# A 3-D affine grid: shared table instructions, one store per add, and theta loaded in halves

## Chip, cores, metric

The kernel runs on one core of one Trainium2 chip. The metric is the device time of one execution in microseconds (us). All times quoted are medians; every execution used here was at a granted clock of 1.0. The span of the profile (first to last recorded instruction) is about 1.8 us shorter than the measured time.

## The reference

For each of 8 batches there is a 3x4 matrix theta. The output at depth z, height y, width x is theta times (x, y, z, 1), with all coordinates running from -1 to 1:

```python
batch, d, h, w = 8, 32, 64, 64
grid = stack([xx, yy, zz, ones], axis=-1)           # d, h, w, 4
result[b] = einsum('dhwc,ec->dhwe', grid, theta[b])  # 8, 32, 64, 64, 3 in float32: 12.58 MB
```

The input is 384 bytes, the output 12.58 MB. The work is to write the output.

## The kernel before

The 256 pairs (batch, depth) are the rows of two tiles of 128 partitions, "half 0" (batches 0 to 3) and "half 1" (batches 4 to 7). Within a partition, every output element is a sum of two table entries: `yc[h, e]` (which also holds the depth and the constant term) and `xt[w, e]`. VectorE builds half 0's tables, ScalarE half 1's. Then VectorE adds them with broadcasts, a few rows of `h` at a time, and stores go out on the sync queue (half 0) and the scalar queue (half 1).

```python
for k in range(2):                       # theta, 32 copies of each batch's 12 numbers
    th_in = dataclasses.replace(theta2d, offset=theta2d.offset + 48 * k,
                                ap=[[12, 4], [0, 32], [1, 12]])
    (nc.sync if k == 0 else nc.scalar).dma_start(out=th[:], in_=th_in)
# ... iota, xrow (x coordinates), zc (z coordinate of each partition, in four blocks of 32)
for e in range(E):                       # half 0's tables: nine small instructions
    nc.vector.tensor_scalar(out=zb0[:, e:e+1], in0=zc[:], scalar1=th0[:, 4*e+2:4*e+3],
                            scalar2=th0[:, 4*e+3:4*e+4], op0=MUL, op1=ADD)
for e in range(E):
    nc.vector.tensor_scalar(out=yc0_3[:, :, e], in0=xrow[:, :H], scalar1=th0[:, 4*e+1:4*e+2],
                            scalar2=zb0[:, e:e+1], op0=MUL, op1=ADD)
    nc.vector.tensor_scalar(out=xt0_3[:, :, e], in0=xrow[:], scalar1=th0[:, 4*e:4*e+1], ...)
# ... half 1's tables, the same on nc.scalar
csplit = [2, 2, 4, 8, 8, 8, 8, 8, 8, 8]  # rows of h in each add
dsplit = [2, 2, 4, 16, 16, 16, 8]        # rows of h in each store
for k in range(2):
    for nh in csplit:
        nc.vector.tensor_tensor(out=otv[:, h0:h0+nh], in0=yc3 (broadcast), in1=xt3 (broadcast), op=ADD)
    q = nc.sync if k == 0 else nc.scalar
    for nh in dsplit:
        q.dma_start(out=out2d[k*P:(k+1)*P, ...], in_=ot[:, ...])
```

## Time and profile before

| | before |
|---|---|
| measured time | 43.54 us |
| span of the profile | 41.7 us |
| first table instruction of half 0 | 4.34 us |
| first add | 6.18 us |
| first output byte starts | 7.61 us |
| VectorE ends its last add | about 33.25 us |
| last output byte | 40.54 us |

The first and the last output byte come from the trace's records of single DMA packets; the rest from the views below.

The page of the kernel before, in 40 slices of the span: busy tenths of VectorE and of the 16 DMA engines, and what they moved, and then the count of packets by size.

```profile
DVE  0400899999999999999999999999999800000000
DMA  0000000785048999899998999998998999889960
GB/s 0 0 8 4 0 0 0 249 305 200 0 188 377 377 518 424 377 389 506 424 377 377 430 402 371 390 480 377 471 471 377 377 506 436 377 377 436 412 283 0
DMA packets 2280, 12.60 MB, mean 302 GB/s; under 512 B 488, under 2 KB 1000, under 8 KB 1512
```

The DMA row is nearly full from the 13th slice to the 38th, while VectorE falls idle seven slices before the DMA engines do. So the stores bound the end, though the page's chain of waits (the chain of work that ended last, followed back) puts 65% of the span on VectorE. There is a gap at the start of the DMA row. In windows of 0.5 us (window, length, busy time of VectorE, ScalarE and GpSimd with instruction counts, clock, DMA share, GB/s) it looks like this:

```profile
7.50:8.00 0.50, 0.50 (x1) 0.00 (x0) 0.00 (x0) 1.00 0.75 261
8.50:9.00 0.50, 0.50 (x1) 0.00 (x0) 0.00 (x0) 1.00 0.54 197
...
9.50:10.00 0.50, 0.50 (x2) 0.00 (x0) 0.00 (x0) 1.00 0.85 332
10.00:10.50 0.50, 0.50 (x1) 0.00 (x0) 0.00 (x0) 1.00 0.00 0
...
11.50:12.00 0.50, 0.50 (x1) 0.00 (x0) 0.00 (x0) 1.00 0.00 0
12.00:12.50 0.50, 0.50 (x1) 0.00 (x0) 0.00 (x0) 1.00 0.94 393
```

Nothing moves for 2 us, because the first 16-row store waits for two adds of 8 rows. The timeline of the sync queue shows when it was issued (start in us, length, what), and the queue's own waits come after it (what waited, for what, total, times, longest):

```profile
11.45 0.33 SPq L137 DMA_DIRECT2D out_dram<-ot  x1
```

```profile
SPq L137 <- DVE ot L130: 16.0, 6, 5.3
```

The store before it was issued from 8.11 to 8.44 us, so the queue waited 3.0 us for the two adds.

The start, from the timeline of the kernel before (start in us, length, engine, line, instruction; in brackets the idle time before it and what ended it):

```profile
0.73 0.71 SPq L47 DMA_DIRECT2D th<-in_theta_dram  x1
0.74 1.09 ACTq L47 DMA_DIRECT2D th<-in_theta_dram  x1
...
4.34 0.27 DVE L90 TENSOR_SCALAR xt<-xrow,th 128x64 f32<-128x64 f32 x1 [2.64 <-DMA th<-in_theta_dram]
...
6.18 27.07 DVE L130 TENSOR_TENSOR ot<-yc,xt 128x384 f32<-128x384 f32 x20
```

The chain of waits has theta's landing for VectorE at 0.73 + 3.51 = 4.24 us (start, length, what):

```profile
0.73 3.51 DMA th<-in_theta_dram
```

VectorE waits 2.64 us for theta, then needs 1.84 us for the tables. The adds by shape (the grouped view with shapes kept apart):

```profile
L130 DVE TENSOR_TENSOR ot<-yc,xt 128x1536 f32<-128x1536 f32 x14 | 23.5, 1750 | 0.0
L130 DVE TENSOR_TENSOR ot<-yc,xt 128x384 f32<-128x384 f32 x4 | 2.0, 551 | 0.0
```

By these two shapes an add costs about 0.15 us plus 1.04 ns per element.

### The profile page before, as it was taken

The page shows a single profiled execution, that of the slowest core. Times are in us where ns is not written, and L with a number is a line of the kernel's source. Part 1 is how long each engine was busy: PE and PEld are TensorE (multiplying, and loading weights), DVE is VectorE, ACT ScalarE, POOL GpSimd, SP SyncE. Part 2 cuts the span into 40 slices and gives each one's busy share as a digit, 9 for nine tenths or more (in the row PEclk, how much of TensorE's full clock was granted, in tenths as well). Part 3 has the DMA queues.
Part 4 walks back from the last instruction along what each step waited for, and adds up shares of the span by engine and source line. Part 5 has one row for each costly group of instructions (what it writes and reads, how often), then busy time and mean ns, then how long its engine had stood idle before and what let it go on. Part 6 is the DMA issues. An engine that isn't in the chain of part 4 may idle for free.

```text
span 41.7 us, 122 instructions
## 1 busy us (share of the span) xinstructions
DVE 29.4 (70%) x32; ACT 4.1 (10%) x11; POOL 1.0 (2%) x9
## 2 busy tenths in 40 slices
DVE  0400899999999999999999999999999800000000
ACT  0297990000000000000000000000000000000000
POOL 4500000000000000000000000000000000000000
DMA  0000000785048999899998999998998999889960
GB/s 0 0 8 4 0 0 0 249 305 200 0 188 377 377 518 424 377 389 506 424 377 377 430 402 371 390 480 377 471 471 377 377 506 436 377 377 436 412 283 0
DMA packets 2280, 12.60 MB, mean 302 GB/s; under 512 B 488, under 2 KB 1000, under 8 KB 1512
## 3 DMA queue, kind: packets, MB, share of 16 engines
q1 hardware_dynamic: 1140, 6.30, 36.9%
q10 hardware_dynamic: 1140, 6.30, 36.7%
HBM read 0.01 MB, written 12.58 MB: 302 GB/s over the span
## 4 chain that ended last, share of the span: by engine, by line
DVE 65%; DMA 8%; DVEq 4%; issue 1%
DVE ot L130 61%; DMA th<-in_theta_dram 8%; DVEq L171 4%; DVE yc L86 2%; DVE zb L81 2%; DVE xt L90 1%; DVEq L90 0%
## 5 line engine op out<-in xcount | busy, mean ns | idle before, releaser
L130 DVE TENSOR_TENSOR ot<-yc,xt 128x1536 f32<-128x1536 f32 (+2 forms) x20 | 27.1, 1430 | 0.0
L90 DVE TENSOR_SCALAR xt<-xrow,th 128x64 f32<-128x64 f32 x3 | 0.8, 268 | 2.6 <-DMA th<-in_theta_dram 2.6
L97 ACT ACT_TABLE_LOAD x1 | 1.3, 1283 | 1.9 <-issue 1.9
L109 ACT ACTIVATE yc<-xrow,zb,th 128x64 f32<-128x64 f32 x3 | 1.2, 456 | 0.0
L112 ACT ACTIVATE xt<-xrow,th 128x64 f32<-128x64 f32 x3 | 1.1, 364 | 0.0
L68 DVE TENSOR_SCALAR xrow<-iw 128x64 f32<-128x64 int32 x1 | 0.2, 195 | 1.1 <-POOL iw L53 1.1
L104 ACT ACTIVATE zb<-zc,th 128x1 f32<-128x1 f32 x3 | 0.9, 372 | 0.0
L86 DVE TENSOR_SCALAR yc<-xrow,th,zb 128x64 f32<-128x64 f32 x3 | 0.9, 324 | 0.0
L81 DVE TENSOR_SCALAR zb<-zc,th 128x1 f32<-128x1 f32 x3 | 0.6, 267 | 0.0
L59 POOL TENSOR_SCALAR zc<-ipf 32x1 f32<-32x1 f32 x2 | 0.4, 182 | 0.2
L59 DVE TENSOR_SCALAR zc<-ipf 32x1 f32<-32x1 f32 x2 | 0.3, 147 | 0.1
L97 ACT ACTIVATE warm<-th 128x12 f32<-128x12 f32 x1 | 0.2, 212 | 0.2 <-DMA th<-in_theta_dram 0.2
L55 POOL CAST ipf<-ip 128x1 f32<-128x1 int32 x1 | 0.2, 212 | 0.1
L53 POOL IOTA iw<- 128x64 int32 x1 | 0.2, 181 | 0.0
L51 POOL IOTA ip<- 128x1 int32 x1 | 0.1, 133 | 0.4 <-PEq L171 0.4
L157 POOL MEMSET const-float32-0.0<- 128x1 f32 x1 | 0.1, 99 | 0.2 <-issue 0.2
L157 POOL MEMSET const-bfloat16-1.0<- 128x1 bf16 x1 | 0.1, 102 | 0.0
L157 POOL MEMSET const-uint8-127<- 128x1 uint8 x1 | 0.1, 102 | 0.0
L157 POOL MEMSET const-float32-1.0<- 128x1 f32 x1 | 0.1, 99 | 0.0
## 6 DMA issues: line engine op xcount, KB each, us to landing
out_dram<-ot SPq DMA_DIRECT2D x3, 1536.0 KB, 5.3
out_dram<-ot ACTq DMA_DIRECT2D x3, 1536.0 KB, 7.1
out_dram<-ot SPq DMA_DIRECT2D x1, 768.0 KB, 6.4
out_dram<-ot ACTq DMA_DIRECT2D x1, 768.0 KB, 7.6
out_dram<-ot SPq DMA_DIRECT2D x2, 192.0 KB, 1.9
out_dram<-ot SPq DMA_DIRECT2D x1, 384.0 KB, 2.3
out_dram<-ot ACTq DMA_DIRECT2D x2, 192.0 KB, 6.1
out_dram<-ot ACTq DMA_DIRECT2D x1, 384.0 KB, 6.0
```

The lines of the kernel that those rows point to most:

```text
L53: nc.gpsimd.iota(iw[:], pattern=[[1, W]], base=0, channel_multiplier=0)
L59: eng.tensor_scalar(out=zc[j * D:(j + 1) * D], in0=ipf[j * D:(j + 1) * D], scalar1=2.0 / (D - 1), scalar2=-1.0 - (2.0 * j * D) / (D - 1), ...
L81: nc.vector.tensor_scalar(out=zb0[:, e:e + 1], in0=zc[:], scalar1=th0[:, 4 * e + 2:4 * e + 3], scalar2=th0[:, 4 * e + 3:4 * e + 4], op0=MU ...
L86: nc.vector.tensor_scalar(out=yc0_3[:, :, e], in0=xrow[:, :H], scalar1=th0[:, 4 * e + 1:4 * e + 2], scalar2=zb0[:, e:e + 1], op0=MUL, op1=ADD)
L90: nc.vector.tensor_scalar(out=xt0_3[:, :, e], in0=xrow[:], scalar1=th0[:, 4 * e:4 * e + 1], scalar2=None, op0=MUL)
L97: nc.scalar.mul(out=warm[:], in_=th1[:], mul=1.0)
L104: nc.scalar.activation(out=zb1[:, e:e + 1], in_=zc[:], func=ident, bias=th1[:, 4 * e + 3:4 * e + 4], scale=th1[:, 4 * e + 2:4 * e + 3])
L109: nc.scalar.activation(out=yc1_3[:, :, e], in_=xrow[:, :H], func=ident, bias=zb1[:, e:e + 1], scale=th1[:, 4 * e + 1:4 * e + 2])
L112: nc.scalar.activation(out=xt1_3[:, :, e], in_=xrow[:], func=copyf, bias=0.0, scale=th1[:, 4 * e:4 * e + 1])
L130: nc.vector.tensor_tensor(out=otv[:, h0:h0 + nh], in0=in0, in1=in1, op=ADD)
L157: nc = _bacc.Bacc("TRN2", target_bir_lowering=False, num_devices=1)
L171: with _tile.TileContext(nc) as tc:
```

## The change

The intent was to reach the first store sooner and then never to let the stores run dry. It has three parts: theta in four half loads spread over both queues; five tensor-tensor instructions for half 0's tables in place of nine per-component ones; adds and stores of the same 4 to 9 rows. (It also adds switchable forms of half 1's tables, which are not used, and moves the z coordinate to VectorE.)

```diff
-        th_in = dataclasses.replace(
-            theta2d, offset=theta2d.offset + 48 * k,
-            ap=[[12, 4], [0, 32], [1, 12]])
-        (nc.sync if k == 0 else nc.scalar).dma_start(out=th[:], in_=th_in)
+        for half in range(2):
+            th_in = dataclasses.replace(
+                theta2d, offset=theta2d.offset + 48 * k + 24 * half,
+                ap=[[12, 2], [0, 32], [1, 12]])
+            q = nc.sync if half == 0 else nc.scalar
+            q.dma_start(out=th[64 * half:64 * (half + 1), :], in_=th_in)
 ...
-    (zc by four blocks of 32 partitions, on GpSimd and VectorE)
+    nc.vector.tensor_scalar(out=ipd[:], in0=ip[:], scalar1=D - 1,
+                            scalar2=None, op0=mybir.AluOpType.bitwise_and)
+    nc.vector.tensor_scalar(out=zc[:], in0=ipd[:], scalar1=2.0 / (D - 1),
+                            scalar2=-1.0, op0=MUL, op1=ADD)
 ...
-    (nine tensor_scalar for zb0, yc0, xt0)
+    nc.vector.tensor_tensor(out=xt0_3[:], in0=xrow_he, in1=thcol(th0, 0), op=MUL)
+    nc.vector.tensor_tensor(out=zb0[:], in0=zc_e, in1=(th0, column 2), op=MUL)
+    nc.vector.tensor_tensor(out=zb0[:], in0=zb0[:], in1=(th0, column 3), op=ADD)
+    nc.vector.tensor_tensor(out=yc0_3[:], in0=xrow_he, in1=thcol(th0, 1), op=MUL)
+    nc.vector.tensor_tensor(out=yc0_3[:], in0=yc0_3[:], in1=(zb0, broadcast), op=ADD)
 ...
-    csplit = [2, 2, 4, 8, 8, 8, 8, 8, 8, 8]
-    dsplit = [2, 2, 4, 16, 16, 16, 8]
+    csplit=(4, 4, 4, 4, 5, 5, 6, 7, 8, 9, 8),
+    dsplit=(4, 4, 4, 4, 5, 5, 6, 7, 8, 9, 8),
```

More of the change, by code (lines that the diff above doesn't have):

```diff
@@ L19 @@
     out: bass.AP,
+    csplit=(4, 4, 4, 4, 5, 5, 6, 7, 8, 9, 8),
+    dsplit=(4, 4, 4, 4, 5, 5, 6, 7, 8, 9, 8),
+    k1_mode="scalar",
+    dma_q="alt",
 ):
@@ L53 @@
     nc.gpsimd.iota(iw[:], pattern=[[1, W]], base=0, channel_multiplier=0)
-    ipf = const.tile([P, 1], fp32)
-    nc.gpsimd.tensor_copy(out=ipf[:], in_=ip[:])
+    ipd = const.tile([P, 1], i32)
+    nc.vector.tensor_scalar(out=ipd[:], in0=ip[:], scalar1=D - 1,
+                            scalar2=None, op0=mybir.AluOpType.bitwise_and)
     zc = const.tile([P, 1], fp32)
-    def zc_block(eng, j):
-        eng.tensor_scalar(
-            out=zc[j * D:(j + 1) * D], in0=ipf[j * D:(j + 1) * D],
-            scalar1=2.0 / (D - 1), scalar2=-1.0 - (2.0 * j * D) / (D - 1),
-            op0=MUL, op1=ADD)
-    zc_block(nc.gpsimd, 0)
-    zc_block(nc.gpsimd, 1)
+    nc.vector.tensor_scalar(out=zc[:], in0=ipd[:], scalar1=2.0 / (D - 1),
+                            scalar2=-1.0, op0=MUL, op1=ADD)
     xrow = const.tile([P, W], fp32)
@@ L69 @@
                             scalar2=-1.0, op0=MUL, op1=ADD)
-    zc_block(nc.vector, 2)
-    zc_block(nc.vector, 3)
     tables = []
@@ L79, with thcol @@
     xt0_3 = xt0.rearrange("p (w e) -> p w e", e=E)
-    for e in range(E):
-        nc.vector.tensor_scalar(
-            out=zb0[:, e:e + 1], in0=zc[:],
-            scalar1=th0[:, 4 * e + 2:4 * e + 3],
-            scalar2=th0[:, 4 * e + 3:4 * e + 4], op0=MUL, op1=ADD)
-    for e in range(E):
-        nc.vector.tensor_scalar(
-            out=yc0_3[:, :, e], in0=xrow[:, :H],
-            scalar1=th0[:, 4 * e + 1:4 * e + 2],
-            scalar2=zb0[:, e:e + 1], op0=MUL, op1=ADD)
-        nc.vector.tensor_scalar(
-            out=xt0_3[:, :, e], in0=xrow[:],
-            scalar1=th0[:, 4 * e:4 * e + 1], scalar2=None, op0=MUL)
+    xrow_he = xrow[:, :, None].to_broadcast((P, W, E))
+    def thcol(th, c):
+        return dataclasses.replace(
+            th, offset=th.offset + c, ap=[th.ap[0], [0, W], [4, E]])
+    nc.vector.tensor_tensor(out=xt0_3[:], in0=xrow_he, in1=thcol(th0, 0),
+                            op=MUL)
+    zc_e = zc.to_broadcast((P, E))
+    nc.vector.tensor_tensor(
+        out=zb0[:], in0=zc_e,
+        in1=dataclasses.replace(th0, offset=th0.offset + 2,
+                                ap=[th0.ap[0], [4, E]]), op=MUL)
+    nc.vector.tensor_tensor(
+        out=zb0[:], in0=zb0[:],
+        in1=dataclasses.replace(th0, offset=th0.offset + 3,
+                                ap=[th0.ap[0], [4, E]]), op=ADD)
+    nc.vector.tensor_tensor(out=yc0_3[:], in0=xrow_he, in1=thcol(th0, 1),
+                            op=MUL)
+    nc.vector.tensor_tensor(
+        out=yc0_3[:], in0=yc0_3[:],
+        in1=zb0[:, None, :].to_broadcast((P, W, E)), op=ADD)
     tables.append((yc0_3, xt0_3))
     th1 = ths[1]
-    warm = const.tile([P, 12], fp32)
-    nc.scalar.mul(out=warm[:], in_=th1[:], mul=1.0)
     zb1 = const.tile([P, E], fp32)
@@ L102, with k1_tables_scalar @@
     xt1_3 = xt1.rearrange("p (w e) -> p w e", e=E)
-    for e in range(E):
-        nc.scalar.activation(
-            out=zb1[:, e:e + 1], in_=zc[:], func=ident,
-            bias=th1[:, 4 * e + 3:4 * e + 4],
-            scale=th1[:, 4 * e + 2:4 * e + 3])
-    for e in range(E):
-        nc.scalar.activation(
-            out=yc1_3[:, :, e], in_=xrow[:, :H], func=ident,
-            bias=zb1[:, e:e + 1], scale=th1[:, 4 * e + 1:4 * e + 2])
-        nc.scalar.activation(
-            out=xt1_3[:, :, e], in_=xrow[:], func=copyf,
-            bias=0.0, scale=th1[:, 4 * e:4 * e + 1])
+    def k1_tables_scalar():
+        warm = const.tile([P, 12], fp32)
+        nc.scalar.mul(out=warm[:], in_=th1[:], mul=1.0)
+        for e in range(E):
+            nc.scalar.activation(
+                out=zb1[:, e:e + 1], in_=zc[:], func=ident,
+                bias=th1[:, 4 * e + 3:4 * e + 4],
+                scale=th1[:, 4 * e + 2:4 * e + 3])
+        for e in range(E):
+            nc.scalar.activation(
+                out=yc1_3[:, :, e], in_=xrow[:, :H], func=ident,
+                bias=zb1[:, e:e + 1], scale=th1[:, 4 * e + 1:4 * e + 2])
+            nc.scalar.activation(
+                out=xt1_3[:, :, e], in_=xrow[:], func=copyf,
+                bias=0.0, scale=th1[:, 4 * e:4 * e + 1])
@@ new lines, in k1_tables_vector @@
+    def k1_tables_vector():
+        for e in range(E):
+            nc.vector.tensor_scalar(
+                out=zb1[:, e:e + 1], in0=zc[:],
+                scalar1=th1[:, 4 * e + 2:4 * e + 3],
+                scalar2=th1[:, 4 * e + 3:4 * e + 4], op0=MUL, op1=ADD)
+        for e in range(E):
+            nc.vector.tensor_scalar(
+                out=yc1_3[:, :, e], in0=xrow[:, :H],
+                scalar1=th1[:, 4 * e + 1:4 * e + 2],
+                scalar2=zb1[:, e:e + 1], op0=MUL, op1=ADD)
+            nc.vector.tensor_scalar(
+                out=xt1_3[:, :, e], in0=xrow[:],
+                scalar1=th1[:, 4 * e:4 * e + 1], scalar2=None, op0=MUL)
@@ new lines, in k1_tables_eng @@
+    def k1_tables_eng(eng):
+        th1_he = thcol(th1, 1)
+        nc_e = eng
+        nc_e.tensor_tensor(out=xt1_3[:], in0=xrow_he, in1=thcol(th1, 0),
+                           op=MUL)
+        nc_e.tensor_tensor(
+            out=zb1[:], in0=zc_e,
+            in1=dataclasses.replace(th1, offset=th1.offset + 2,
+                                    ap=[th1.ap[0], [4, E]]), op=MUL)
+        nc_e.tensor_tensor(
+            out=zb1[:], in0=zb1[:],
+            in1=dataclasses.replace(th1, offset=th1.offset + 3,
+                                    ap=[th1.ap[0], [4, E]]), op=ADD)
+        nc_e.tensor_tensor(out=yc1_3[:], in0=xrow_he, in1=th1_he, op=MUL)
+        nc_e.tensor_tensor(
+            out=yc1_3[:], in0=yc1_3[:],
+            in1=zb1[:, None, :].to_broadcast((P, W, E)), op=ADD)
@@ L115 @@
     tables.append((yc1_3, xt1_3))
-    csplit = [2, 2, 4, 8, 8, 8, 8, 8, 8, 8]
-    dsplit = [2, 2, 4, 16, 16, 16, 8]
+    if k1_mode == "scalar":
+        k1_tables_scalar()
+    elif k1_mode == "gpsimd":
+        k1_tables_eng(nc.gpsimd)
     assert sum(csplit) == H and sum(dsplit) == H
@@ L126 @@
         h0 = 0
-        for nh in csplit:
+        for ci, nh in enumerate(csplit):
             in0 = yc3[:, h0:h0 + nh, None, :].to_broadcast((P, nh, W, E))
@@ L132 @@
             h0 += nh
-        q = nc.sync if k == 0 else nc.scalar
+            if k == 0 and ci == 4 and k1_mode == "vector":
+                k1_tables_eng(nc.vector)
+        if dma_q == "alt":
+            q = nc.sync if k == 0 else nc.scalar
+        elif dma_q == "scalar":
+            q = nc.scalar
+        else:
+            q = nc.sync
         h0 = 0
```

## The prediction

> **What bounds the kernel now.** The output stores, and the time before they are fed. In windows of 0.5 us, the DMA share is 0.9 or more from 12.0 us to about 40.4 us: 11.80 MB in 28.4 us, 416 GB/s. VectorE ends its last add at 33.25 us, 7 us before the last byte; the chain of waits gives VectorE 65%, but its adds outrun the DMA (one 128x1536 add per 1.67 us: 786 KB, 470 GB/s). So the end is first output byte (7.6 us) + bytes/rate + holes. The holes, in the same windows: nothing moves from 10.0 to 12.0 us, because the 16-row store waits for two 8-row adds (sync queue's waits on VectorE: longest 5.3 us); 8.5 to 9.0 us runs at half rate. The first 0.79 MB takes 2.4 us.
>
> **Start.** Theta lands for VectorE at about 4.24 us. Nine small VectorE instructions run 4.34 to 6.18 us, then a 0.55 us add, and bytes 0.87 us after its end.
>
> **What the change does.**
> 1. Tables of half 0: nine instructions (1.84 us) become five tensor-tensor ones, three of 192 elements, two of 3. Adds cost 551 ns at 384 and 1749 at 1536, hence about 0.35 us at 192 and 0.16 at 3 (estimate[...]). With overlaps of 0.08 us, 1.17 us: saves 0.67. The first add is 768 wide, not 384: +0.40. Net 0.27 us earlier.
> 2. Stores of 4 to 9 rows, one per add: the hole vanishes; 4-row adds (0.87 us apart, 393 KB, 450 GB/s) outrun the DMA. Smaller rows are less efficient: DMA share against GB/s gives about 391 GB/s for 3 KB rows, 410 for 6 KB, 422 for 12 KB. I take 408: 30.8 us for all, against 32.8 us now.
> 3. Theta in four half loads. [...] The trace agrees on 4: 488 packets under 512 B are 256 theta rows + 14x16 + 2x4. Two engines carry what four did; theta 0 waits behind as many rows per engine as now: landing 4.2 us +- 0.4, no gain. Theta 1 lands later (5 to 6 us); needed near 20 us.
> 4. zc on VectorE, and ScalarE's table load waiting for theta 1: in slack.
> 5. Eight completion semaphores serve 22 stores; reuse waits for one eight back, long landed. No cost.
>
> **Time.** First byte near 7.3 us, last near 38.1 against 40.36: -2.25 us. 43.54 - 2.25 = about 41.2 us (40.4 to 42.1). Faster by over 2%: 0.88; within 2%: 0.11; slower: 0.01.
>
> **What would show it.** Windows: no empty one between first and last byte; DMA rate 405 to 415; first byte 7.0 to 7.7 us. First add about 1.2 us after the first table instruction. Packets under 512 B: 256 + 22x16 + 4x2 = 616 if two engines carry each load. VectorE's adds unchanged in sum (27.2 us).
>
> **What would make it wrong.** Theta landing much later, if one queue starves the other on two engines (at worst all 256 rows first, about 6 us, +1.8 us, leaving a 1% gain); small stores well under 400 GB/s[...].

The sum came to -2.27 us (tables -0.67, wider first add +0.40, stores -2.0, theta 0) and is given as -2.25. The estimate of 0.35 us at 192 elements and 0.16 at 3 follows from 551 ns at 384 and 1749 at 1536. The number of engines that carry a load: that it is four now, the trace shows (each theta load has four packets of 4 bytes beside its 128 rows); that it would be two after was my assumption. On it rest the 0 for theta and the 5 to 6 us: estimates, the latter of which fits twice the 1.80 us of all 256 rows in the kernel before (2.11 to 3.91), hence 5.7. The trace has 1.04 ns per element. The overlap of 0.08 us is the trace's: the 20 adds are 28.6 us long one by one and took 27.07.

## The result and the profile after

The changed kernel takes 40.95 us (8 runs, 40.94 to 40.97) against 43.55 us for the kernel before (13 runs). The ratio is 0.9401, with a 95% interval of 0.9392 to 0.9411: 6% faster. A ratio here is the mean time of one kernel's fast runs over that of the other's of the same rounds, so it is not quite the ratio of the medians.

| | before | after | difference |
|---|---|---|---|
| measured time | 43.55 us | 40.95 us | -2.60 |
| span of the profile | 41.7 us | 39.2 us | -2.5 |
| first table instruction | 4.34 us | 3.76 us | -0.58 |
| from there to the first add | 1.84 us | 1.20 us | -0.64 |
| first output byte | 7.61 us | 6.80 us | -0.81 |
| first to last output byte | 32.93 us | 31.08 us | -1.85 |
| last output byte | 40.54 us | 37.87 us | -2.67 |
| from there to the end of the span | 1.19 us | 1.35 us | +0.16 |

The page of the changed kernel, the same rows as shown of before:

```profile
DVE  0301999999999999999999999999999980000000
DMA  0000000999999999999999999999999999999940
GB/s 0 0 4 6 2 0 28 395 401 395 406 403 396 410 414 433 412 414 418 402 389 439 376 404 398 401 406 403 403 407 421 406 424 407 429 402 416 414 163 0
DMA packets 3432, 12.60 MB, mean 321 GB/s; under 512 B 616, under 2 KB 616, under 8 KB 3432
```

The gap is gone. The count of packets under 512 B is the predicted 616: 256 rows of theta and 360 packets of 4 bytes, 16 for each of 22 stores and two for each half load, where a whole load had four before. So, with one such packet for each engine, two engines carry each half load. In windows of 0.5 us, two of the stretches that were empty or half empty before:

```profile
8.50:9.00 0.50, 0.50 (x2) 0.00 (x0) 0.00 (x0) 1.00 1.04 406
...
10.00:10.50 0.50, 0.50 (x1) 0.00 (x0) 0.00 (x0) 1.00 1.01 393
```

The start, from the timeline of the changed kernel:

```profile
0.73 1.40 SPq L53 DMA_DIRECT2D th<-in_theta_dram  x2
0.74 1.65 ACTq L53 DMA_DIRECT2D th<-in_theta_dram  x2
...
3.76 0.36 DVE L84 TENSOR_TENSOR xt<-xrow,th 128x192 f32<-128x192 f32 x1 [2.39 <-DMA th<-in_theta_dram]
...
4.57 0.36 DVE L97 TENSOR_TENSOR yc<-yc,zb 128x192 f32<-128x192 f32 x1
4.96 27.20 DVE L175 TENSOR_TENSOR ot<-yc,xt 128x768 f32<-128x768 f32 x22
```

The chain of waits has the landing at 0.73 + 2.90 = 3.63 us now:

```profile
0.73 2.90 DMA th<-in_theta_dram
```

The tables take the predicted time, and the adds' total is unchanged (27.20 us against 27.07). But theta is there 0.58 us sooner, and that was not predicted. So the time came from three places: the hole, the tables, and the landing of theta.

### The profile page after: what moved, and what is told of

Its sections match the earlier page's. It is cut to its first block, busy times and chain, and to the rows that moved or that the text cites. A ratio compares the mean times of both kernels' runs of the same rounds, so it can differ in the third digit from the quotient of the medians.

```text
span 39.2 us, 137 instructions
## 1 busy us (share of the span) xinstructions
DVE 28.7 (73%) x30; ACT 4.1 (10%) x11; POOL 0.5 (1%) x6
## 3 DMA queue, kind: packets, MB, share of 16 engines
q1 hardware_dynamic: 1716, 6.30, 40.4%
## 4 chain that ended last, share of the span: by engine, by line
DVE 70%; DMA 7%; DVEq 2%; issue 0%
DVE ot L175 67%; DMA th<-in_theta_dram 7%; DVEq L223 2%; DVE yc L97 1%; DVE xt L84 1%; DVE yc L95 1%; DVE zb L91 0%; DVE zb L87 0%; DVEq L84 0%
## 5 line engine op out<-in xcount | busy, mean ns | idle before, releaser
L175 DVE TENSOR_TENSOR ot<-yc,xt 128x768 f32<-128x768 f32 (+5 forms) x22 | 27.2, 1316 | 0.0
```

The source lines that it names most:

```text
L175: nc.vector.tensor_tensor(out=otv[:, h0:h0 + nh], in0=in0, in1=in1, op=ADD)
```

## The experiments

All nine gave correct results (no e6 is on record). Those named together ran on the same chip, beside the same runs of the kernel before (43.55 us; 43.57 us beside e10, which ran alone on another chip). e1 and e2 lie within 2% of the kernel before, but their intervals lie clear of 1, so the small gains are real.

| kernel | time | ratio to before (95%) |
|---|---|---|
| e1, only the theta halves | 43.12 | 0.9902 (0.9887 to 0.9917) |
| e2, only the tables | 42.90 | 0.9853 (0.9838 to 0.9868) |
| e3, only the splits | 42.08 | 0.9672 (0.9651 to 0.9693) |
| e4, changed, whole loads, theta 0 on scalar | 40.82 | 0.9373 (0.9358 to 0.9389) |
| e5, changed, half 1's stores merged | 40.60 | 0.9329 (0.9312 to 0.9346) |
| e7, e4 with depth outermost | 41.80 | 0.9602 (0.9588 to 0.9616) |
| e8, e4 with growing stores | 40.16 | 0.9232 (0.9207 to 0.9256) |
| e9, theta spread by TensorE, growing stores | 39.27 | 0.9027 (0.9012 to 0.9042) |
| e10, e4 with the batch halves exchanged | 40.56 | 0.9313 (0.9289 to 0.9336) |

### e1, e2, e3: each part alone (with e4 on one chip)

Each takes one part of the diff above over into the kernel before, and nothing else.

e1, the theta halves:

> The kernel before with only the four half loads of theta. Theory A (each queue hands out theta rows at its own pace, about 105 rows per us on the sync queue whether two or four engines carry them; half a load there means 64 rows instead of 128): the last row of theta 0 lands 0.6 us earlier, the first table instruction starts at about 3.75 us instead of 4.34, everything behind moves with it: about 42.95 us. Theory B (my prediction: pace is set by rows per engine): no gain, about 43.5 us; the early start seen after the change would then come from something else.

e2, the tables:

> The kernel before with only the five tensor-tensor instructions for the tables of half 0 (and zc on VectorE). If the tables are worth what they shorten the run-up by, first table instruction at 4.34 us as before, first add 1.18 us later instead of 1.84, hole of 2 us unchanged: 43.54 - 0.66 = about 42.9 us. Rival (the hole absorbs it, the stores being bound elsewhere): about 43.5 us.

e3, the splits:

> The kernel before with only the new splits of the adds and stores. First add 0.40 us longer, so first byte near 8.0 us; then no hole, 31.1 us from first to last byte as in the changed kernel, last byte near 39.1 instead of 40.5: 43.54 - 1.4 = about 42.1 us. If the three parts add up, the three gains sum to about 2.6 us; a sum well under that would mean that one part hides another.

The first instruction of the tables and the first add in each, from the timelines of e1, e2 and e3 in this order:

```profile
3.77 0.27 DVE L92 TENSOR_SCALAR xt<-xrow,th 128x64 f32<-128x64 f32 x1 [2.06 <-DMA th<-in_theta_dram]
...
5.61 3.56 DVE L132 TENSOR_TENSOR ot<-yc,xt 128x384 f32<-128x384 f32 x4
```

```profile
4.37 0.36 DVE L78 TENSOR_TENSOR xt<-xrow,th 128x192 f32<-128x192 f32 x1 [2.99 <-DMA th<-in_theta_dram]
...
5.57 3.56 DVE L131 TENSOR_TENSOR ot<-yc,xt 128x384 f32<-128x384 f32 x4
```

```profile
4.39 0.27 DVE L90 TENSOR_SCALAR xt<-xrow,th 128x64 f32<-128x64 f32 x1 [2.68 <-DMA th<-in_theta_dram]
...
6.23 2.70 DVE L130 TENSOR_TENSOR ot<-yc,xt 128x768 f32<-128x768 f32 x3
```

- e1 gains 0.43 us: the halves alone bring the earlier landing (3.77 us), so theory B (my prediction's step) falls. The gain is less than the 0.57 us of the landing. The last byte moved by 0.55 us (40.54 to 39.99), but the end of the program got 0.16 us longer (see e4).
- e2 gains 0.65 us, as expected: from the first table instruction to the first add 1.20 us instead of 1.84, and the hole behind absorbs nothing of it.
- e3 gains 1.47 us, as expected: first byte at 8.06 us (later, for the longer first add), then 31.05 us to the last byte, as in the changed kernel.
- 0.43 + 0.65 + 1.47 = 2.55 us, against 2.60 us for the whole change: the parts add up. None hides another.

### e4: which load of theta goes first

```diff
-        for half in range(2): (two half loads, one per queue)
+        th_in = dataclasses.replace(theta2d, offset=theta2d.offset + 48 * k,
+                                    ap=[[12, 4], [0, 32], [1, 12]])
+        (nc.sync if k == 1 else nc.scalar).dma_start(out=th[:], in_=th_in)
```

> The changed kernel with theta in two whole loads again, but with the load of half 0 on the scalar queue and that of half 1 on the sync queue. Theory A2 (the scalar queue's rows start at 2.1 us, the sync queue's at 2.7 us, whichever load it is): the 128 rows of theta 0 are done at 3.0 us, before the 3.3 us of the half loads; first table instruction at about 3.45 us instead of 3.76; about 40.65 us. Rival (the load that the program issues first gets going second, whichever queue it is on): rows from 2.7 to 3.9 us, first table instruction at 4.3 us, about 41.5 us.

Neither number came out. The first table instruction is at 3.77 us, as with the half loads (3.76):

```profile
0.73 0.71 SPq L51 DMA_DIRECT2D th<-in_theta_dram  x1
0.74 1.10 ACTq L51 DMA_DIRECT2D th<-in_theta_dram  x1
...
3.77 0.36 DVE L82 TENSOR_TENSOR xt<-xrow,th 128x192 f32<-128x192 f32 x1 [2.39 <-DMA th<-in_theta_dram]
```

The traces' records of the 48-byte packets, one for each row of theta, explain the two kernels. They give, for each queue, when its theta rows ran (which load a row belongs to follows from its queue and its place in it):

| kernel | scalar queue | sync queue | rows of theta 0 done |
|---|---|---|---|
| before | theta 1: 2.11 to 3.02 us | theta 0: 2.71 to 3.91 | 3.91 |
| after | theta 0, 64 rows: 2.11 to about 2.71; theta 1, 64 rows: 3.84 to 4.14 | theta 0, 64 rows: 2.71 to about 3.31; theta 1, 64 rows: to 3.91 | 3.31 |
| e4 | theta 0: 2.13 to 3.33 | theta 1: 3.28 to 3.92 | 3.33 |

The scalar queue's rows go first in each of these, and the sync queue's first row comes 0.02 to 0.14 us after the scalar queue's first 4-byte packet, of which a whole load has four and a half load two (2.62 us in the kernel before, 2.69 after, 3.14 in e4). In the kernel before the scalar queue's rows are theta 1's, which no add needs before 19.76 us, and theta 0 starts behind the first of them. In the changed kernel and in e4 theta 0's 128 rows are the first that are served. And those 128 rows take 1.20 us in all three, about 106 rows per us (the expectations say 105), whether on one queue or two, on two engines a load or on four (by the counts of 4-byte packets). So the half loads win by putting theta 0 ahead of theta 1, not by splitting it, and e4 gets the same by exchanging two queues.

e4 is even a little faster than the changed kernel (40.82 against 40.95 us; that one was measured in another call) though its last byte lands at the same time (37.86 against 37.87). The span ends 1.18 us after the last byte instead of 1.35. In the trace, the sync engine waits for the DMA semaphores one after another in a fixed order at the end. In the changed kernel (26 DMAs over 8 semaphores) the last store's semaphore is not the last in that order, and three more waits of about 62 ns each follow it (at 38.28, 38.34 and 38.40 us); in e4 (24 DMAs) the last store's wait is the last. e1 shows the same lengthening from 1.19 to 1.35 us.

### e5: what a row of a store costs

```diff
-        for nh in dsplit:
+        for nh in (dsplit if k == 0 else (8, 8, 10, 13, 17, 8)):
```

> The changed kernel, its adds untouched, with the eleven stores of half 1 merged into six (8, 8, 10, 13, 17, 8 rows). Theory: a row of a store costs its engine a fixed 11 ns besides its bytes (from the mean packet times of 126 ns at 3 KB, 239 at 6 KB and 467 at 12 KB in the kernel before). Five stores fewer are 5 x 8 = 40 rows fewer per engine, 0.44 us less from first to last byte: 40.95 - 0.44 = about 40.5 us. Rival (only bytes count while the queue is fed): unchanged, 40.95 us within 0.1.

From first to last byte it took 30.64 us instead of 31.08: 0.44 us less, the expected number. The measured time is 0.35 us lower, since its end after the last byte is 1.38 us, with three waits after the last store's as in the changed kernel. So a store's row costs its engine about 11 ns besides its bytes. Every store here has 8 rows for each engine (128 rows and 16 packets of 4 bytes), so e5 alone can't tell a cost for each row from one of about 90 ns for each store. The means of single packets, one for each row, can, and they give the cost for each row: in the kernel before, 126 ns for 3 KB, 239 for 6 KB and 467 for 12 KB, hence 0.037 ns a byte plus 11 to 13 ns.

### e7: more engines for theta (with e5, e8 and e9 on one chip)

```diff
-            ap=[[12, 4], [0, 32], [1, 12]])
+            ap=[[0, 32], [12, 4], [1, 12]])
 ...
-    ipd = ip & 31                      # partition = 32 * batch + depth
+    ipd = ip >> 2                      # partition = 4 * depth + batch
 ...
-                out=out2d[k * P:(k + 1) * P, h0 * W * E:h0 * W * E + F],
+                out=(out2d, offset + 4 * k * D * ROW + h0 * W * E,
+                     ap=[[ROW, D], [D * ROW, 4], [1, F]]),
```

> The changed kernel with theta in two whole loads (half 0 on the scalar queue) and with the rows of a tile reordered so that depth is the outer and batch the inner index of the partitions: [...] 16 engines carry it (under 512 B 256 + 22x16 + 2x16 = 640 packets). Theory (a few engines working through their rows one by one are the limit): 8 rows an engine, the 128 rows of theta 0 done within 0.3 us of the first, first table instruction near 2.9 us instead of 3.77, about 40.0 us. Rival (the rows, all of them reads of the same 192 bytes, are handed out at about 105 per us whatever the number of engines): 1.2 us as before, first table instruction at about 3.75 us, about 40.8 us. Should the stores get slower by the new row order, the first and last byte will tell it apart.

The page of e7 counts the expected 640 packets under 512 B (256 + 22x16 + 2x16), so a load has 16 packets of 4 bytes, as a store has: 16 engines carry it. The timeline shows a late start all the same:

```profile
DMA packets 3456, 12.60 MB, mean 314 GB/s; under 512 B 640, under 2 KB 640, under 8 KB 3456
```

```profile
4.49 0.36 DVE L83 TENSOR_TENSOR xt<-xrow,th 128x192 f32<-128x192 f32 x1 [3.12 <-DMA th<-in_theta_dram]
```

Both expected times missed, in the same direction. By the packets, theta 0's rows ran from 2.85 to 4.05 us: 1.20 us again, about 106 rows per us, now on 16 engines. That is what the rival said. The late start has another cause: this time the sync queue's rows, theta 1's, went first (2.25 to 3.06 us). Why the order of the two queues turned round stays open. The stores were not hurt by the new row order: 30.99 us from first to last byte.

### e10: what sets the pace of theta's rows

```diff
-            theta2d, offset=theta2d.offset + 48 * k,
+            theta2d, offset=theta2d.offset + 48 * (1 - k),
 ...
-                out=out2d[k * P:(k + 1) * P, ...],
+                out=out2d[(1 - k) * P:(2 - k) * P, ...],
```

> The kernel e4 with the two halves of the batch exchanged: the tile that is computed first holds batches 4 to 7, so the load on the scalar queue reads theta at byte 192 to 383 and the one on the sync queue at 0 to 191; nothing else changes. So far the 128 rows of batches 0 to 3 always took 1.2 us (105 rows per us), on either queue and with 2, 4 or 16 engines, and those of batches 4 to 7 about 0.9 us. Theory (the pace goes with what is read): the first tile's rows are done in about 0.9 us, 3.0 us instead of 3.33, first table instruction at about 3.45 us, about 40.5 us. Rival (the pace goes with which load is served first, or with its place in the program): 1.2 us again, first table instruction at 3.77 us, 40.8 us.

```profile
3.48 0.36 DVE L82 TENSOR_TENSOR xt<-xrow,th 128x192 f32<-128x192 f32 x1 [2.11 <-DMA th<-in_theta_dram]
```

The theory held. Rows of batches 4 to 7 took 0.87 us (2.17 to 3.04) on the same queue, in the same place, where those of batches 0 to 3 took 1.20 us in e4: about 147 rows per us against 106. So the pace depends on what is read. But that is not all it depends on: the rows of batches 0 to 3 took 1.20 us in every run that copies them 32 times, while those of batches 4 to 7 took 0.91 us in the kernel before and 0.81 in e7, where they were served first, and only 0.64 in e4 (200 rows per us), where they were served second. The expectation's "about 0.9 us" left e4's out. By which mechanism, whether the place of those bytes in memory or something else about them, no run here shows.

### e8 and e9: a faster version

e8 is e4 with one split for each half:

```diff
-    csplit=(4, 4, 4, 4, 5, 5, 6, 7, 8, 9, 8),   # both halves
+    csplit=((3, 4, 4, 5, 6, 7, 8, 9, 9, 9), (13, 15, 17, 19)),
```

> The kernel e4 (theta 0 on the scalar queue) with adds and stores that start at 3 rows and grow to 19: 14 stores instead of 22. Theory: first add 0.20 us shorter than with 4 rows; 8 x 8 = 64 rows fewer per engine at 11 ns, 0.70 us; about 0.1 us of holes by my sums: last byte 0.78 us earlier than in the changed kernel, about 40.05 to 40.2 us. Rival (only bytes count): 0.2 us at most, about 40.7 us.

e8 came out at 40.16 us, in the expected range: first byte at 6.63 us, 30.56 us to the last. Part of this hit is luck: the last byte (37.19 us) came 0.68 us earlier than in the changed kernel, not the expected 0.78, and the end after it is 0.17 us shorter, which the expectation does not name. The stores can grow because VectorE gains on the queue with every row: a row takes VectorE about 0.20 us (192 elements at 1.04 ns) and the queue 0.24 (98.3 KB at the changed kernel's 405 GB/s).

e9 replaces the copies made by the load:

```diff
-    (two loads of 128 rows)
+    thall = const.tile([B, 12], fp32)
+    nc.sync.dma_start(out=thall[:], in_=theta2d)          # 8 rows
+    (sel[b, p] = 1 where p // 32 == b, from an iota and is_equal, while waiting)
+    for k in range(2):
+        th = psum.tile([P, 12], fp32, name=f"th_{k}")
+        nc.tensor.matmul(th[:], sel[:, k * P:(k + 1) * P], thall[:], start=True, stop=True)
 ...
+    csplit=((3, 4, 4, 5, 6, 6, 7, 8, 10, 11), (12, 12, 12, 16, 12)),
```

> As e8 (splits 3 to 11 and 12 to 16 rows, 15 stores), but theta comes in one load of 8 rows, and TensorE spreads it to the 128 partitions by a product with a 0/1 matrix. Theory: the replicated load is what the start waits for (256 rows at about 105 per us); 8 rows land about 0.4 us after 2.1 us, [...]first table instruction near 2.9 us instead of 3.77: about 39.3 us. Rival (the fixed delay of a load, not its rows, sets the landing): first table instruction not before 3.6 us, about 40.1 us or slower.

Its sum of 2.9 us: 2.1 and 0.4 us for the eight rows, the rest a guess for TensorE, of which no run had shown anything by then. The 0.4 us is an estimate that the kernel before bears out: 8 rows at 105 per us, 0.08 us, and 0.33 us from the last row (3.91) to the landing (4.24).

```profile
0.74 0.39 SPq L47 DMA_DIRECT2D thall<-in_theta_dram  x1
...
2.17 0.92 PEld L62 LDWEIGHTS th<-thall,sel 8*128 8x128 f32 x4 [2.17 <-DVE sel L57]
2.21 0.99 PE L62 MATMUL th<-thall,sel 8*128 8x12 f32 x4 [2.21 <-DMA thall<-in_theta_dram]
2.81 0.35 DVE L89 TENSOR_TENSOR xt<-xrow,th 128x192 f32<-128x192 f32 x1 [1.11 <-PE th L62]
```

For comparison, the same instruction in e8:

```profile
3.79 0.36 DVE L81 TENSOR_TENSOR xt<-xrow,th 128x192 f32<-128x192 f32 x1 [2.42 <-DMA th<-in_theta_dram]
```

The eight rows start at 1.68 us, earlier than the expected 2.1, and are done by 1.75; TensorE begins at 2.21, and the tables at 2.81 us instead of 3.79 in e8. TensorE and its handover thus took 0.60 us. The first output byte is at 5.76 us, the last at 36.28. At 39.27 us, 9.7% below the kernel before, e9 beats both kernels.

## Why the prediction was right or wrong

"Faster by over 2%" and the time (41.2 us, range 40.4 to 42.1; measured 40.95) were right, but one step was wrong, the landing of theta. It was worth 0.6 us, and part of it was cancelled by other errors. That the time came within 0.25 us was luck; that it fell into the range was not, since the landing alone would have moved the sum only to about 40.7 us (41.29 - 0.58; the sum is at the end of this section).

- **The bound: right.** After the hole was closed the stores ran from 6.80 to 37.87 us without an empty window, and e3 got 1.47 us from the splits alone, though the chain of waits gives VectorE 70% of the span. The first stores, of 4 rows (393 KB), held 387 to 406 GB/s from 7.0 to 9.0 us. For the stretch from first to last byte I predicted 32.8 to 30.8 us; it went from 32.93 to 31.08 us (405 GB/s, the lower edge of the predicted 405 to 415).
- **The sum behind it.** The smaller stores cost 0.70 us more, by e5's 11 ns: 2816 rows instead of 1792 are 64 more for each of 16 engines. So the holes were worth about 1.85 + 0.70 = 2.55 us (an estimate from these, not measured alone).
- **The tables: right.** 1.17 us was predicted, 1.20 measured, and e2 alone is worth 0.65 us. An add over 192 elements took 0.35 to 0.36 us with strided, broadcast operands, as estimated from the longer adds of the kernel before (0.15 us + 192 x 1.04 ns = 0.35).
- **Engine count: right, its consequence wrong.** The 488, 616 and 640 small packets fit 4, 2 and 16 engines for a load before, after and in e7; beforehand the 2 and the 16 were my assumption. The failed step is "theta 0 waits behind as many rows per engine as now: landing 4.2 us +- 0.4, no gain". In its place the runs showed that the rows for each engine did not set the pace: theta 0 came at about 106 rows per us on 2, 4 or 16 engines (after, e4, e7). What changed was the order of service: before, theta 1's rows were ahead of theta 0's; after, theta 0's are first. The landing came to 3.63 us in the chain of waits, against 4.24 before. This moved the first byte to 6.80 us, outside the predicted 7.0 to 7.7.
- **Theta 1 "5 to 6 us": wrong, without effect.** Its rows were done at 4.14 us, and ScalarE, which waited for it, was released at 4.29.
- **Semaphores "no cost": wrong by a little.** Reuse of the 8 semaphores cost nothing (the changed kernel's stores on the sync queue waited only for VectorE, 11 times), but the waits at the program's end grew by 0.16 us (after, e1).

The predicted change of -2.25 us was off by -0.6 us for theta, by about +0.15 us in the stretch from first to last byte (-1.85 instead of -2.0) and by +0.16 us at the end, so that part of the miss was cancelled. (43.54 - 2.25 is 41.29; the prediction says "about 41.2".)

## What to carry to other kernels

When stores bound a kernel, compare its first output byte and the empty windows of the DMA before looking at busy shares: a store that needs two adds can leave a hole while it waits for them (here 2 us), and stores that grow as fast as the compute engine gains ground can leave none (here 4 to 9 rows, no empty window from 6.80 to 37.87 us). Ask of every load ahead of the first byte whether a load that is needed later is served before it, and whether it must replicate data: 8 rows and a small product with a 0/1 matrix had the tables begin about 1 us sooner than 256 replicated rows (2.81 us in e9, 3.79 in e8). Count what a smaller store costs in fixed time per row (here about 11 ns) before cutting everything small; only the first few need to be.
